# A two-layer decoder trunk on one core: the first stage taken by column quarters with one accumulator each, and residuals of the next projections queued behind the first keys

## The chip, the cores and the metric

The kernel runs on one core of one Trainium2 chip. The metric is the device time of one execution in microseconds (us); before the change it is 693.19 us, the median of 3 runs (692.89 to 694.17).

## The reference, cut to what matters

Two layers over x of shape (1, 256, 1024), all in float32. Each layer is conditioned by `ada = silu(c) @ w_ada + b_ada`, cut into six vectors of 1024 (shift, scale and gate, twice).

```python
def reference(...):
    for l in range(2):
        sh1, sc1, g1, sh2, sc2, g2 = split(silu(c) @ w_ada[l] + b_ada[l], 6)
        h = x * (1.0 + sc1) + sh1
        y = mixer_ab(h, ...) if l == 0 else mixer_cd(h, ...)     # two kinds of attention heads, then @ w_o[l]
        x = layer_norm(ALPHA * x + (1.0 + g1) * y, ln_g[l, 0], ln_b[l, 0])
        h = x * (1.0 + sc2) + sh2
        y = swiglu(h, w_ffn_in[l], w_ffn_out[l])                 # width 2816
        x = layer_norm(ALPHA * x + (1.0 + g2) * y, ln_g[l, 1], ln_b[l, 1])
    return x
```

Layer 0 mixes differential attention (queries q1, keys k1, values v1; a second softmax map is subtracted with a factor lambda made from `diff_lambda`) and dilated window attention (q2, k2, v2). Layer 1 mixes block attention and forgetting attention. All weights, some 160 MB, are read once.

## The kernel before, in words

**Pieces.** Every weight matrix comes in pieces of 128 partitions x 1024 float32 (0.524 MB). The list `stream` holds all of them in the order in which they are to be loaded. `load_ahead` (L76) issues their transfers on SyncE's queue (SP) into a ring of `NR` = 10 raw buffers; `next_piece` (L90) takes the next entry: for a projection weight it makes two tiles by `split` (L72), a rounded copy `hi` (cast on ScalarE, L73) and the residual `lo` (a subtraction on VectorE, L74), and for an `ada` weight it multiplies the piece by a column of silu(c) and adds it to an accumulator on VectorE. Each product of the reference is then three matmuls: hi by hi, lo by hi, hi by lo (`mm3`, L389 to L391, `unit_t_q`, L447 to L449). `piece(name, q)` takes entries until the one asked for is there. After the first stage `room["ring"]` is 7: `pump` takes entries ahead until that many weight pieces are split and not yet used, and `used` pumps again. Those instructions are traced at a lower priority (`high_priority(offset=-LOW)`).

**Order.** Outside of `tc.manual_schedule()` a scheduler orders each engine's instructions by priority and by its own estimate of time; inside, and on SP always, they stay in the order of the program. Engines run their queues in order. Instructions traced later may be put between those of the first stage.

**The first stage** (L607 on) makes h = x(1+sc1)+sh1 and layer 0's v10, q10 and k10 in four quarters q of 256 columns. For a quarter, `first_entries` (L307) streams four pieces of scale and shift weights, each holding two of the eight k of the contraction; VectorE keeps two accumulators, one for even and one for odd k (L317, L319). `first_cols` (L574) sums them over partitions with matmuls against ones (`fin`, L579; two for each of four columns of 128; a float32 matmul shows as two records) and transposes x (`xT`, L585); `first_h` (L589) adds the bias (`column`, L254), forms `hf` on VectorE (L595) and splits it into h. Then come the three projections of that quarter into six PSUM banks, in the order v10, q10 of quarter q, `fin` of q+1, k10 of q, and the splits of v10 of q+1. In `stream` a quarter is four ada pieces, then v10, q10, k10; x and the layer norms' vectors are loaded after the first four pieces, and the small tables, with a bias table, before the last k10. After the fourth quarter `evac_q1` and `evac_k1` copy the queries and keys out of PSUM (the first half of the keys on VectorE, the second on ScalarE, L477), and v1 follows on ScalarE (L636). `bias_vectors` (L557) at the start waits for a table, `kbt`, that ScalarE's queue loads.

**After it**, `attend_diff` (L718) runs layer 0's first attention as 12 steps woven with the projections q20 and k20, two units of six matmuls a step (`weave`). The score banks (0 and 1) are those that held k10. The softmax's exponential is L666 on ScalarE; step s scores map s and makes the softmax of map s-1. `lambdas` (L195) forms lambda before the weave.

**The norm** (`Norm`, L848): `stats` makes the residual sum, its statistics, the reciprocal root on GpSimd (`rsqrt1`, L545) and scales the row's halves, one on ScalarE (L901) and one on VectorE (L902); `turn` transposes, `fill` makes the next h.

Of the kernel before, what the change touches and what calls it, by code (L numbers as in the profile page):

```python
# [2 lines left out]

# [6 lines left out]
F32 = mybir.dt.float32  # L10
# [29 lines left out]
def trunk(ctx, tc, x, c, rel_bias, w_ada, b_ada, ln_g, ln_b, w_in_ab, diff_lambda,  # L40
# [17 lines left out]
    def s4(shape, name, dt=F32):  # L58
# [10 lines left out]
    room = {"ring": 0}  # L69
    at = {"dma": 0, "done": 0, "made": 0, "used": 0}  # L70

    def split(hi, lo, src):  # L72
        A.copy(hi, src)  # L73
        V.tensor_tensor(lo, src, hi.bitcast(F32), OP.subtract)  # L74

    def load_ahead():  # L76
        while at["dma"] < len(stream) and at["dma"] - at["done"] < NR:
# [9 lines left out]
                nc.sync.dma_start(dst, src)  # L87
            at["dma"] += 1

    def next_piece():  # L90

        if at["dma"] == at["done"]:
            load_ahead()
        e = stream[at["done"]]
        if "load" not in e:
            with tc.high_priority(offset=-LOW if room["ring"] else 0):
                if "key" in e:
                    n = "_".join(map(str, e["key"]))
# [6 lines left out]
                    split(hi, lo, e["raw"])  # L105
# [71 lines left out]
    lams = const.tile([128, 2], F32, name="lams")  # L177
    nlam = const.tile([128, 1], F32, name="nlam")

    def load_x():  # L180
        nc.sync.dma_start(rows, b_ada.rearrange("l (i p) -> (l i) p", p=128))
        for t in range(2):
            nc.sync.dma_start(xt[t], x[0, tok(t), :])
        nc.sync.dma_start(lnr[0:32, :], ln_g.rearrange("l i (k p) -> (l i k) p", p=128))
        nc.sync.dma_start(lnr[32:64, :], ln_b.rearrange("l i (k p) -> (l i k) p", p=128))

# [8 lines left out]
    def lambdas():  # L195

        for i in range(2):
            V.scalar_tensor_tensor(lamr[:, 4], lamr[:, 2 * i], 1.0, lamr[:, 2 * i + 1],
                                   OP.mult, OP.mult, accum_out=lams[:, i:i + 1])
# [3 lines left out]
        V.tensor_scalar(subln, subln, 1.0 - LAMBDA_INIT, None, OP.mult)  # L203


    bcol = const.tile([128, 96], F32, name="bcol")
# [100 lines left out]
    def first_entries(q):  # L307
        def work_of(a):
            def go(raw):
                r = raw.rearrange("p (j n) -> p j n", j=2)  # L310
                if a == 0:
                    first[q] = s4([128, 2, 512], f"acc_q{q}")
                for j in range(2):
                    k = 2 * a + j
                    acc = first[q][:, j]
                    if a == 0:
                        V.tensor_scalar(acc, r[:, j], c_sb[:, k:k + 1], None, OP.mult)  # L317
                    else:
# [12 lines left out]
        for a in range(4):  # L331
            stream.append({"work": work_of(a), "dmas": dmas_of(a)})
        for n, c0 in (("v10", 1024), ("q10", 0), ("k10", 512)):
            stream.append(cols_entry(w_in_ab[0], c0, q, n))

    fdw = []

# [33 lines left out]
        stream.extend(rest)  # L371

    for q in range(4):
        first_entries(q)
    stream[4:4] = [{"load": load_x}]
    stream[28:28] = [{"load": load_small}, bias_entry(0)]
    chunk = lambda *ls: [e for l, i in ls for e in ada_entries(l, i)]
    attn0, ffn0 = layer_entries(0)
    attn1, ffn1 = layer_entries(1)
# [20 lines left out]
    def tok(t):  # L400
        return slice(t * 128, t * 128 + 128)
# [63 lines left out]
    def keys(name, E=(A.copy, A.copy)):  # L465

        dst = [s4([128, 4, T], f"{name}{b2}") for b2 in range(2)]
        halves = [d.rearrange("p (b e) t -> p b e t", e=2) for d in dst]
        for d in halves:
            for e in range(2):  # L470
                G.memset(d[64 - e * 64:128 - e * 64, :, e], 0.0)

        def evac(ps, b2):
            p3 = ps.rearrange("p (b t) -> p b t", b=2)
            for e in range(2):
                own = slice(e * 64, e * 64 + 64)
                E[e](halves[b2][own, :, e], p3[own])  # L477

        return dst, evac

# [76 lines left out]
    def bias_vectors():  # L557
        for i in range(2):
# [3 lines left out]
            A.copy(bv, bps[0:8, 0:NV])  # L562
            G.dma_start(vecs[8 * i:8 * i + 8, :], bv)

    h = new_h("00")
    psv = [bank(3, "v10p0"), bank(5, "v10p1")]
    psq = [bank(4, "q10p0"), bank(6, "q10p1")]
    psk = [bank(0, "k10p0"), bank(1, "k10p1")]
# [5 lines left out]
    def first_cols(q):  # L574

        ps = bank(2, f"fin{q}")
        for k in range(4):
            for j in range(2):
                PE.matmul(ps[:, k:k + 1], sums[q][:, j, k * 128:(k + 1) * 128], ones[:, 0:1],  # L579
                          start=j == 0, stop=j == 1)  # L580
        xp = bank(7, f"xT{q}")
        for t in range(2):
            for k in range(2):
                kk = 2 * q + k
                PE.transpose(xp[:, k * 256 + t * 128:k * 256 + t * 128 + 128],  # L585
                             xt[t][:, kk * 128:(kk + 1) * 128], ident)
        return ps, xp

    def first_h(q, ps, xp):  # L589
        column(ps[:, 0:2], 2, 0, 1, 2 * q, f"a{q}")  # L590
        column(ps[:, 2:4], 2, 0, 0, 2 * q, f"b{q}")
        hf = work.tile([128, 2, T], F32, tag="hf", name=f"hf{q}", bufs=2)
        for k in range(2):
            kk = 2 * q + k
            V.tensor_scalar(hf[:, k], xp[:, k * 256:k * 256 + 256], ada[0, 1][:, kk:kk + 1],  # L595
                            ada[0, 0][:, kk:kk + 1], OP.mult, OP.add)
        sl = slice((q % 2) * 2, (q % 2) * 2 + 2)
        split(h[0][q // 2][:, sl], h[1][q // 2][:, sl], hf)

    def qkv(name):  # L600
        return s4([128, 1024], name)
# [3 lines left out]
    k1, evac_k1 = keys("k1", (V.tensor_copy, A.copy))  # L605
    tps = bank(2, "colps")
    with tc.manual_schedule():  # L607
        bias_vectors()
        first_sums(0)
        PE.transpose(tps[:, 0:96], rows, ident[0:96, 0:96])  # L610
        A.copy(bcol, tps[:, 0:96])
        cols = first_cols(0)
        for q in range(4):
            first_h(q, *cols)
            piece("v10", q)
            piece("q10", q)
            for t in range(2):
                run(unit_q(psv[t], "v10", h, t, q, t == 1))
            if q == 3:
# [3 lines left out]
            piece("k10", q)  # L623
            for b2 in range(2):
                run(unit_t_q(psq[b2], "q10", h, b2, q, b2 == 1))
            if q < 3:
                first_sums(q + 1)
                cols = first_cols(q + 1)
                piece("v10", q + 1)
            for b2 in range(2):  # L630
                run(unit_t_q(psk[b2], "k10", h, b2, q, b2 == 1))
        for b2 in range(2):
            evac_q1(psq[b2], b2)
            evac_k1(psk[b2], b2)
        for t in range(2):
            A.copy(v1[:, t], psv[t])  # L636

    room["ring"] = NW // 2
    pump()


    HALF = (slice(0, 128), slice(128, 384))
# [205 lines left out]
    class Norm:  # L848
# [30 lines left out]
        def stats(self, t, ps):  # L879
# [42 lines left out]
        def fill(self, t):  # L922
            for q in range(2):
                hf = work.tile([128, 4, 128], F32, tag="hf", name="hf", bufs=2)
                for k in range(4):
# [121 lines left out]
    for l in range(DEPTH):  # L1047
# [132 lines left out]
```

## Time and profile before

| | |
|---|---|
| runs, median (lowest to highest) | 693.19 us (692.89 to 694.17) |
| the profiled execution, its own time | 693.62 us |
| its span, first to last instruction | 691.6 us |
| TensorE busy | 656.9 us, 95% |
| VectorE busy | 499.8 us, 72% |
| ScalarE busy | 351.3 us, 51% |
| GpSimd busy | 55.2 us, 8% |
| moved by the transfers | 163.21 MB, mean 236 GB/s |

The profile is of one execution. Times are counted from the first instruction of the span. An engine's instructions are named by line, operation and tile; PE is TensorE, DVE VectorE, ACT ScalarE, SP SyncE. The bracket behind an instruction says how long the engine was idle before it and what ended that. A granted clock of 1.00 is 2.4 GHz, 0.50 is 1.2 GHz.

### The profile page before, as it was taken

What the parts mean: (1) busy time and instruction counts of PE and PEld (TensorE: products, weight loads), DVE (VectorE), ACT (ScalarE), POOL (GpSimd) and SP (SyncE); (2) the same over time, 40 slices, a digit from 0 to 9 for tenths busy, and PEclk for the clock granted to TensorE, in tenths of its full rate; (3) what the DMA queues carried; (4) which work ended last, traced back from release to release, by engine and by line L of the source; (5) the groups of instructions that cost most, each with busy time, mean ns of one, the idle gap of its engine ahead of it and who ended that gap; (6) DMA issues with size and microseconds to landing.
All of it is one profiled execution on the core that took longest, in us unless ns stands there. A gap on an engine that the chain in (4) does not pass through costs nothing.

```text
span 691.6 us, 11460 instructions
## 1 busy us (share of the span) xinstructions
PE 656.9 (95%) x4300; PEld 594.4 (86%) x4300; DVE 499.8 (72%) x782; ACT 351.3 (51%) x615; POOL 55.2 (8%) x98
## 2 busy tenths in 40 slices
PE   4899999998999999999999999999799999999994
PEld 2788998877998999999878899978689999999884
DVE  3787999967977787586788868566776558555375
ACT  1426877835544434443557469765564444444330
POOL 4000001011100000000127100100200000000002
PEclk9999999999999999999999999999999999999997
DMA  9999798943899979788846857823466777765101
GB/s 301 360 365 361 250 335 334 343 145 122 305 340 328 321 268 314 225 311 241 271 157 229 297 201 234 280 96 109 140 201 217 225 225 248 238 223 186 32 1 61
DMA packets 96627, 163.21 MB, mean 236 GB/s; under 512 B 8299, under 2 KB 64539, under 8 KB 96572
## 3 DMA queue, kind: packets, MB, share of 16 engines
q1 hardware_dynamic: 95856, 161.82, 70.1%
q8 instruction: 33, 0.54, 0.3%
q10 hardware_dynamic: 524, 0.63, 0.3%
q14 instruction: 22, 0.18, 0.1%
q0 software_dynamic: 192, 0.04, 0.0%
HBM read 161.39 MB, written 1.07 MB: 235 GB/s over the span
## 4 chain that ended last, share of the span: by engine, by line
PE 82%; DVE 7%; DMA 5%; issue 3%; POOL 2%; ACT 1%; DVEq 0%; POOLq 0%; SPq 0%; ACTq 0%
PE gu L432 10%; PE gu L431 10%; PE gu L429 10%; PE f L389 6%; PE f L390 6%; PE f L391 6%; PE gu L389 2%; PE gu L391 2%; PE gu L390 2%; PE y L389 1%; PE y L391 1%; PE y L390 1%; DMA raw<-in_w_ada_dram 1%; PE fin L579 1%; PE adp L279 1%
## 5 line engine op out<-in xcount | busy, mean ns | idle before, releaser
L429 PE MATMUL gu<-h,hifi 128*128 128x256 f32 x576 | 163.0, 283 | 0.0
L431 PE MATMUL gu<-h,hifi 128*128 128x256 f32 x576 | 162.9, 283 | 0.0
L432 PE MATMUL gu<-h,lofi 128*128 128x256 f32 x576 | 162.9, 283 | 0.0
L74 DVE TENSOR_TENSOR lofi<-raw,hifi 128x1024 fp32r<-128x1024 f32 x88 | 105.9, 1220 | 25.8 <-PE gu L431 15.7
L235 DVE SCALAR_TENSOR_TENSOR acc<-raw,c_sb,acc 128x1024 f32<-128x1024 f32 x70 | 89.8, 1285 | 30.0 <-DMA raw<-in_w_ada_dram 29.8
L429 PEld LDWEIGHTS gu<-h,hifi 128*128 128x128 f32 x576 | 110.5, 192 | 0.5
L431 PEld LDWEIGHTS gu<-h,hifi 128*128 128x128 f32 x576 | 110.5, 192 | 0.4
L432 PEld LDWEIGHTS gu<-h,lofi 128*128 128x128 f32 x576 | 110.4, 192 | 0.2
L73 ACT CAST hifi<-raw 128x1024 fp32r<-128x1024 f32 x88 | 91.2, 1048 | 27.5 <-PE y L391 14.0
L389 PE MATMUL f<-hifo,hid 128*128 128x512 f32 (+1 forms) x198 | 74.1, 374 | 0.0
L390 PE MATMUL f<-lofo,hid 128*128 128x512 f32 (+1 forms) x198 | 73.4, 371 | 0.0
L391 PE MATMUL f<-hifo,hid 128*128 128x512 f32 (+1 forms) x198 | 72.9, 368 | 0.0
L73 ACT CAST hifo<-raw 128x1024 fp32r<-128x1024 f32 x44 | 46.2, 1051 | 49.0 <-PE f L391 27.2
L74 DVE TENSOR_TENSOR lofo<-raw,hifo 128x1024 fp32r<-128x1024 f32 x44 | 53.8, 1222 | 5.9 <-PE gu L390 2.4
L978 ACT ACTIVATE sg<-gu 128x256 f32<-128x256 f32 x36 | 13.8, 383 | 79.4 <-PE gu L432 79.4
L548 POOL TENSOR_SCALAR b<-mv 128x1 f32<-128x1 f32 x8 | 6.4, 805 | 466.4 <-DVE mv L894 466.4
L390 PEld LDWEIGHTS f<-lofo,hid 128*128 128x128 f32 x198 | 37.4, 189 | 6.8 <-issue 1.2
L389 PEld LDWEIGHTS f<-hifo,hid 128*128 128x128 f32 x198 | 37.4, 189 | 6.8 <-issue 1.0
L391 PEld LDWEIGHTS f<-hifo,hid 128*128 128x128 f32 x198 | 37.3, 188 | 6.8 <-issue 0.7
L979 DVE TENSOR_TENSOR sg<-gu,sg 128x256 f32<-128x256 f32 x36 | 15.1, 421 | 30.3 <-ACT sg L978 30.3
L389 PE MATMUL gu<-hifi,h 128*128 128x512 f32 x64 | 26.4, 413 | 1.8 <-ACT h L73 1.8
L389 PE MATMUL y<-hiwo,o 128*128 128x512 f32 x64 | 26.5, 416 | 0.0
(352 smaller groups left out, 1438.5 us busy)
## 6 DMA issues: line engine op xcount, KB each, us to landing
raw<-in_w_ffn_in_dram SPq DMA_DIRECT2D x176, 256.0 KB, 4.8
raw<-in_w_ada_dram SPq DMA_DIRECT2D x80, 512.0 KB, 5.2
raw<-in_w_ffn_out_dram SPq DMA_DIRECT2D x44, 512.0 KB, 5.5
raw<-in_w_in_ab_dram SPq DMA_DIRECT2D x24, 512.0 KB, 6.6
raw<-in_w_in_cd_dram SPq DMA_DIRECT2D x24, 512.0 KB, 4.9
raw<-in_w_ada_dram SPq DMA_DIRECT2D x32, 256.0 KB, 6.6
raw<-in_w_o_dram SPq DMA_DIRECT2D x16, 512.0 KB, 5.9
bias<-vecs SPq DMA_DIRECT2D x5, 512.0 KB, 6.7
```

Of the source, the lines that this page charges most:

```text
L73: A.copy(hi, src)
L74: V.tensor_tensor(lo, src, hi.bitcast(F32), OP.subtract)
L235: V.scalar_tensor_tensor(acc, raw, ck, box["z"] if k == 0 else acc, OP.mult, OP.add)
L279: PE.matmul(ps[:, k:k + 1], acc[:, k * 128:(k + 1) * 128], ones[:, 0:1], start=True, stop=True)
L389: PE.matmul(ps, xs[0], ws[0], start=first, stop=False, skip_group_check=True)
L390: PE.matmul(ps, xs[0], ws[1], start=False, stop=False, skip_group_check=True)
L391: PE.matmul(ps, xs[1], ws[0], start=False, stop=last, skip_group_check=True)
L429: PE.matmul(p, wh, hh, start=k == 0 and g == 0, stop=False, skip_group_check=True)
L431: PE.matmul(p, wh, hl, start=False, stop=False, skip_group_check=True)
L432: PE.matmul(p, wl, hh, start=False, stop=k == KT - 1, skip_group_check=True)
L978: A.activation(sg, ps[:, 0:256], AF.Silu)
L979: V.tensor_tensor(sg, ps[:, 256:512], sg, OP.mult)
```

## The change

The diff does the following. (1) A quarter of the first stage keeps one accumulator for all eight k, and from quarter 1 on its first product is a ScalarE activation; `fin` needs four matmuls instead of eight. (2) x is loaded by column quarters, each behind its quarter's ada pieces; k10 of a quarter is streamed a quarter later, and the last k10 comes after the small tables. (3) In a quarter, TensorE now does v10, q10 of q, `fin` of q+1, k10 of q; the transposes stand ahead of `fin`. (4) From quarter 1 on `hf` is made by ScalarE; in quarter 0 h is split by columns of 128 and the v10 residual is queued behind the first of them. The v10 split is taken inside `first_h`. (5) TensorE gets six warming matmuls at the start and two behind the first `fin`. (6) The copies out of PSUM at the end of the stage are put between the last matmuls. (7) After the stage two pieces are pumped freely; the others are traced with `tc.issue_after`, which keeps their VectorE instructions behind the VectorE copy of the second key half. The same is done in layer 1's norms, behind the VectorE scaling of a token half. (8) `lambdas` is called in the second step of the attention.

```diff
+    room = {"ring": 0, "after": None}
+    late = []
-    def split(hi, lo, src):
+    def split(hi, lo, src, now=True):
         A.copy(hi, src)
-        V.tensor_tensor(lo, src, hi.bitcast(F32), OP.subtract)
+        late.append(lambda: V.tensor_tensor(lo, src, hi.bitcast(F32), OP.subtract))
+        if now:
+            late.pop()()
...
-    def next_piece():
+    def next_piece(now=True):
...
-            with tc.high_priority(offset=-LOW if room["ring"] else 0):
+            with tc.high_priority(offset=-LOW if room["ring"] else 0), \
+                    tc.issue_after(room["after"]) if room["after"] else nullcontext():
...
-    def load_x():
+    def load_x(q):
...
+        cs = slice(q * 256, (q + 1) * 256)
         for t in range(2):
-            nc.sync.dma_start(xt[t], x[0, tok(t), :])
+            nc.sync.dma_start(xt[t][:, cs], x[0, tok(t), cs])
+        if q == 2:
+            load_ln()
...
-                    first[q] = s4([128, 2, 512], f"acc_q{q}")
+                    first[q] = s4([128, 512], f"acc_q{q}")
+                acc = first[q]
                 for j in range(2):
                     k = 2 * a + j
-                    acc = first[q][:, j]
-                    if a == 0:
+                    if k == 0 and q:
+                        A.activation(acc, r[:, j], AF.Copy, scale=c_sb[:, k:k + 1])
+                    elif k == 0:
                         V.tensor_scalar(acc, r[:, j], c_sb[:, k:k + 1], None, OP.mult)
...
     for q in range(4):
-        first_entries(q)
-    stream[4:4] = [{"load": load_x}]
-    stream[28:28] = [{"load": load_small}, bias_entry(0)]
+        stream += first_entries(q) + [{"load": lambda q=q: load_x(q)}]
+        for n, c0, k in (("k10", 512, q - 1), ("v10", 1024, q), ("q10", 0, q)):
+            if k >= 0:
+                stream.append(cols_entry(w_in_ab[0], c0, k, n))
+    stream += [{"load": load_small}, bias_entry(0), cols_entry(w_in_ab[0], 512, 3, "k10")]
...
+    def warm(n):
+        for _ in range(n):
+            PE.matmul(wps, ones, ones[:, 0:1].to_broadcast([128, 512]), start=True, stop=True)
...
+        for k in range(4):
+            PE.matmul(ps[:, k:k + 1], sums[q][:, k * 128:(k + 1) * 128], ones[:, 0:1],
+                      start=True, stop=True)
...
         column(ps[:, 2:4], 2, 0, 0, 2 * q, f"b{q}")
+        next_piece(q > 0)
...
+            if q:
+                A.activation(hf[:, k], s, AF.Identity, bias=b, scale=g)
+            else:
+                V.tensor_scalar(hf[:, k], s, g, b, OP.mult, OP.add)
+        for k in range(0, 2, 2 if q else 1):
+            ks = slice(k, 2 if q else k + 1)
+            sl = slice((q % 2) * 2 + ks.start, (q % 2) * 2 + ks.stop)
+            split(h[0][q // 2][:, sl], h[1][q // 2][:, sl], hf[:, ks])
+            while late:
+                late.pop()()
...
+        warm(6)
         bias_vectors()
         first_sums(0)
...
         cols = first_cols(0)
+        warm(2)
+        first_h(0, *cols)
+        piece("q10", 0)
...
         for q in range(4):
...
             for t in range(2):
                 run(unit_q(psv[t], "v10", h, t, q, t == 1))
+            q_units(q)
+            if q < 3:
+                first_sums(q + 1)
+                cols = first_cols(q + 1)
+                piece("k10", q)
+                first_h(q + 1, *cols)
+                piece("q10", q + 1)
+            else:
+                piece("k10", q)
...
+                for b2 in range(2):
+                    evac_q1(psq[b2], b2)
             for b2 in range(2):
                 run(unit_t_q(psk[b2], "k10", h, b2, q, b2 == 1))
+                if q == 3:
+                    keyed = evac_k1(psk[b2], b2)
+                if q == 3 and b2 == 0:
+                    A.copy(v1[:, 0], psv[0])
+        A.copy(v1[:, 1], psv[1])
-    room["ring"] = NW // 2
+    room["ring"] = 2
     pump()
+    room["ring"], room["after"] = NW // 2, keyed.ins
+    pump()
+    room["after"] = None
...
-            V.tensor_scalar(r[:, 0:512], r[:, 0:512], mv[:, 0:1], rstd, OP.subtract, OP.mult)
+            half = V.tensor_scalar(r[:, 0:512], r[:, 0:512], mv[:, 0:1], rstd, OP.subtract,
+                                   OP.mult)
+            if l:
+                room["after"] = half.ins
...
+            if t == 1:
+                room["after"] = None
...
-            lambdas()
+            steps[1] = lambda step=steps[1]: (step(), lambdas())
```

## Rows read from the trace of the kernel before

**Rows 1.** Chain of waits, 0 to 110 us: start, us, what, by count.
```profile
3.74 4.96 DMA kbt<-in_k_bucket_dram
...
23.64 0.43 PE v10p L390
...
28.51 1.68 PE fin L579 x16
...
47.15 0.23 PE v10p L389
...
50.25 0.12 PE q10p L447
...
65.53 0.68 DVE k L477
...
68.70 0.46 PE scA L654 x2
...
100.48 0.86 PE gbp L270 x2
```

**Rows 2.** Stretches: length, busy by engine (instructions), granted clock, DMA share, GB/s.
```profile
0.00:69.00 69.00, 54.70 (x333) 47.61 (x334) 47.50 (x78) 24.98 (x34) 10.35 (x25) 0.98 1.02 347
...
25.20:35.30 10.10, 10.10 (x79) 9.72 (x78) 7.49 (x12) 3.59 (x5) 1.04 (x2) 1.00 1.08 362
...
42.60:45.80 3.20, 3.20 (x17) 3.20 (x16) 1.83 (x4) 1.74 (x3) 0.77 (x2) 0.50 1.06 371
...
69.00:80.00 11.00, 11.00 (x88) 10.69 (x86) 9.87 (x34) 10.27 (x29) 0.00 (x0) 1.00 0.70 222
80.00:100.00 20.00, 20.00 (x169) 19.85 (x168) 19.93 (x42) 14.13 (x40) 0.00 (x0) 1.00 0.90 306
100.00:120.00 20.00, 20.00 (x101) 16.13 (x100) 19.48 (x51) 15.34 (x37) 2.35 (x3) 1.00 0.92 348
120.00:140.00 20.00, 20.00 (x107) 16.73 (x107) 18.16 (x31) 15.38 (x40) 0.00 (x0) 1.00 1.03 351
140.00:150.00 10.00, 10.00 (x61) 8.85 (x61) 5.56 (x12) 1.04 (x1) 1.88 (x3) 1.00 0.23 78
```

**Rows 3.** VectorE in order of time, first stage: start, us, line, out<-in.
```profile
10.74 1.42 DVE L319 SCALAR_TENSOR_TENSOR acc_q<-raw,c_sb,acc_q 128x512 f32<-128x512 f32 x2 [0.30 <-DMA raw<-in_w_ada_dram]
...
23.64 4.07 DVE L319 SCALAR_TENSOR_TENSOR acc_q<-raw,c_sb,acc_q 128x512 f32<-128x512 f32 x6
...
30.73 0.99 DVE L595 TENSOR_SCALAR hf<-xT,col,col 128x256 f32<-128x256 f32 x2 [0.27 <-PE xT L585]
32.41 0.69 DVE L74 TENSOR_TENSOR h<-hf,h 128x512 fp32r<-128x512 f32 x1 [0.69 <-ACT h L73]
33.36 1.23 DVE L74 TENSOR_TENSOR loq<-raw,hiq 128x1024 fp32r<-128x1024 f32 x1 [0.26 <-ACT hiq L73]
...
43.03 1.00 DVE L595 TENSOR_SCALAR hf<-xT,col,col 128x256 f32<-128x256 f32 x2 [0.49 <-PE xT L585]
```

**Rows 4.** ScalarE in order of time, first stage.
```profile
25.20 1.05 ACT L73 CAST hiv<-raw 128x1024 fp32r<-128x1024 f32 x1 [3.91 <-DMA raw<-in_w_in_ab_dram]
...
35.28 1.05 ACT L73 CAST hiv<-raw 128x1024 fp32r<-128x1024 f32 x1 [1.00 <-DMA raw<-in_w_in_ab_dram]
...
57.72 1.28 ACT L200 ACT_TABLE_LOAD   x1
...
67.97 0.58 ACT L477 COPY k<-k10p 64x512 f32<-64x512 f32 x1 [0.39 <-DVE k L477]
```

**Rows 5.** VectorE in order of time, layer 1's first norm.
```profile
480.52 1.22 DVE L74 TENSOR_TENSOR lofi<-raw,hifi 128x1024 fp32r<-128x1024 f32 x1
...
482.97 1.18 DVE L74 TENSOR_TENSOR lofi<-raw,hifi 128x1024 fp32r<-128x1024 f32 x1
```

**Rows 6.** TensorE in order of time, around 40 and 487 us.
```profile
39.98 0.35 PE L579 MATMUL fin<-ones,acc_q 128*128 128x1 f32 x2 [0.80 <-DVE acc_q L319]
...
486.71 0.44 PE L920 MATMUL xnT100v<-ident,x 128*128 128x128 f32 x2 [1.88 <-DVE x L902]
```

More of the change, by code (lines that the diff above doesn't have):

```diff
@@ L1 @@
 import math
-from contextlib import ExitStack
+from contextlib import ExitStack, nullcontext
 import concourse.bass as bass
@@ L68, in trunk @@
              ("fo1", 2 * NU - 1)}
-    room = {"ring": 0}
+    room = {"ring": 0, "after": None}
     at = {"dma": 0, "done": 0, "made": 0, "used": 0}
-    def split(hi, lo, src):
+    late = []
+    def split(hi, lo, src, now=True):
         A.copy(hi, src)
-        V.tensor_tensor(lo, src, hi.bitcast(F32), OP.subtract)
+        late.append(lambda: V.tensor_tensor(lo, src, hi.bitcast(F32), OP.subtract))
+        if now:
+            late.pop()()
     def load_ahead():
@@ L104, in next_piece @@
                         at["made"] += 1
-                    split(hi, lo, e["raw"])
+                    split(hi, lo, e["raw"], now)
                     pieces[e["key"]] = (hi, lo)
@@ L178, in trunk, with load_ln @@
     nlam = const.tile([128, 1], F32, name="nlam")
-    def load_x():
-        nc.sync.dma_start(rows, b_ada.rearrange("l (i p) -> (l i) p", p=128))
+    def load_x(q):
+        if q == 0:
+            nc.sync.dma_start(rows, b_ada.rearrange("l (i p) -> (l i) p", p=128))
+        cs = slice(q * 256, (q + 1) * 256)
         for t in range(2):
-            nc.sync.dma_start(xt[t], x[0, tok(t), :])
+            nc.sync.dma_start(xt[t][:, cs], x[0, tok(t), cs])
+        if q == 2:
+            load_ln()
+    def load_ln():
         nc.sync.dma_start(lnr[0:32, :], ln_g.rearrange("l i (k p) -> (l i k) p", p=128))
@@ L197, in lambdas @@
         for i in range(2):
-            V.scalar_tensor_tensor(lamr[:, 4], lamr[:, 2 * i], 1.0, lamr[:, 2 * i + 1],
-                                   OP.mult, OP.mult, accum_out=lams[:, i:i + 1])
+            tc.keep_in_program_order(
+                V.scalar_tensor_tensor(lamr[:, 4], lamr[:, 2 * i], 1.0, lamr[:, 2 * i + 1],
+                                       OP.mult, OP.mult, accum_out=lams[:, i:i + 1]))
         A.activation(lams, lams, AF.Exp)
@@ L202, in lambdas @@
                                OP.subtract)
-        V.tensor_scalar(subln, subln, 1.0 - LAMBDA_INIT, None, OP.mult)
+        tc.keep_in_program_order(V.tensor_scalar(subln, subln, 1.0 - LAMBDA_INIT, None, OP.mult))
     bcol = const.tile([128, 96], F32, name="bcol")
@@ L329, in dmas_of @@
                 for g, i in enumerate((1, 0))]
[L331 to L334, printed above, removed]
+        return [{"work": work_of(a), "dmas": dmas_of(a)} for a in range(4)]
     fdw = []
@@ L476, in evac @@
                 own = slice(e * 64, e * 64 + 64)
-                E[e](halves[b2][own, :, e], p3[own])
+                done = E[e](halves[b2][own, :, e], p3[own])
+                if e == 0:
+                    first = done
+            return first
         return dst, evac
@@ L563, in bias_vectors @@
             G.dma_start(vecs[8 * i:8 * i + 8, :], bv)
+    def warm(n):
+        for _ in range(n):
+            PE.matmul(wps, ones, ones[:, 0:1].to_broadcast([128, 512]), start=True, stop=True)
     h = new_h("00")
+    wps = bank(3, "warm")
     psv = [bank(3, "v10p0"), bank(5, "v10p1")]
@@ L576, in first_cols @@
         ps = bank(2, f"fin{q}")
[L577 to L580, printed above, removed]
         xp = bank(7, f"xT{q}")
@@ L594, in first_h @@
             kk = 2 * q + k
[L595 to L598, printed above, removed]
+            s, g, b = xp[:, k * 256:k * 256 + 256], ada[0, 1][:, kk:kk + 1], ada[0, 0][:, kk:kk + 1]
+            if q:
[8 more added lines that the diff above has]
+                late.pop()()
     def qkv(name):
@@ L612, in trunk, with q_units @@
         cols = first_cols(0)
+        warm(2)
+        first_h(0, *cols)
+        piece("q10", 0)
+        def q_units(q):
+            for b2 in range(2):
+                run(unit_t_q(psq[b2], "q10", h, b2, q, b2 == 1))
         for q in range(4):
-            first_h(q, *cols)
-            piece("v10", q)
-            piece("q10", q)
             for t in range(2):
                 run(unit_q(psv[t], "v10", h, t, q, t == 1))
-            if q == 3:
+            q_units(q)
[7 more added lines that the diff above has]
+                piece("k10", q)
                 tps = bank(7, "lnps")
@@ L622, in trunk @@
                 A.copy(lncol, tps[:, 0:64])
[L623 to L629, printed above, removed]
+                for b2 in range(2):
+                    evac_q1(psq[b2], b2)
             for b2 in range(2):
                 run(unit_t_q(psk[b2], "k10", h, b2, q, b2 == 1))
[L632 to L636, printed above, removed]
-    room["ring"] = NW // 2
+                if q == 3:
[4 more added lines that the diff above has]
+    room["ring"] = 2
     pump()
+    room["ring"], room["after"] = NW // 2, keyed.ins
+    pump()
+    room["after"] = None
     HALF = (slice(0, 128), slice(128, 384))
```

## The prediction

> **What bounds the kernel now.** I read the page's slices first, then busy time by stretch, then the chain of waits, then the queues of VectorE, ScalarE and TensorE in order of time. TensorE is busy 95% of the span, and its idle time lies at the front: 54.70 us busy in the first 69, then 71 of 71 up to 140 [rows 2]. So what is worth asking is when layer 0's attention starts. Its first score pair needs a PSUM bank that still holds the last key sums; the chain shows the second pair starting at 68.70 [rows 1]. From there TensorE is the bound, and a start earlier by d us ends the run d earlier, if VectorE and the transfers keep up.
>
> Up to there, two things run side by side. The transfers are saturated: 347 GB/s over the first 69 us, 362 GB/s at a DMA share above 1 in 25.2 to 35.3 [rows 2]. ScalarE waits for data only at two value pieces, at 25.20 and 35.28 [rows 4]. Between those two arrivals lie seven pieces of 128x1024 f32 (0.524 MB): 3.67 MB in 10.08 us, 0.364 MB/us, 1.44 us a piece. At that pace the first stage's data would be in by 50 us, 19 before it ends. The rest is the order of work: per quarter VectorE does two first products, six accumulations (4.07), three residuals (1.22 each, 1.14 apart), `hf` (0.99) and its residual (0.69) [rows 3], about 10.3 us with the columns, and its waits for ScalarE and TensorE make it 12.3 (`hf` at 30.73, the next at 43.03). TensorE also has 16 one-column records for `fin` (1.68 in quarter 1 [rows 1]).
>
> **First stage, the data.** I count the new order in pieces of 1.44 us, taking x's quarter as half a piece and anchoring on the old order, in which v10 of quarter 1 is the 14th piece and there at 25.1. Then in the new order: weights of ada quarter 1 complete at 20.1, k10 of quarter 0 at 22.2, ada quarter 2 at 30.9, k10 of 1 at 33.0, ada quarter 3 at 41.7, k10 of 2 at 43.8, v10 of 3 at 45.3, q10 of 3 at 46.7. The small loads and a bias table follow (1.35 pieces), so the last, k10 of 3, lands at 50.1, and the four q20 pieces at 51.5 to 55.9. Cutting x into eight transfers adds six issues of about 0.4 us on SP, which is issuing seven or more pieces ahead by then: nothing.
>
> **First stage, the engines.** A quarter is 7.5 pieces, 10.8 us of transfer. TensorE's share of it: 24 matmuls for k and 24 for q at 0.12 (2.88 each), 12 for v at 0.23 (2.76) [rows 1], `fin` now 8 records instead of 16 (1.68/2, so 0.84), transposes 0.5 (from that `fin`'s end at 30.19 to `hf` at 30.73 [rows 3]): 9.9. VectorE, from a key piece's landing: cast 1.04 [rows 4], residual 1.22, columns 0.25 (an estimate: within that same gap), v residual 1.14, a wait of about 0.15 for `hf` and its cast on ScalarE (two 256-column activations, each at most the 0.58 of a 512-column copy [rows 4], beside the v residual), 0.69, q residual 1.14, seven accumulations of 0.68 (4.75): 10.4, so the sums stand 0.4 before the next key piece. The single accumulator makes each step wait for the one before; bounds: nothing, or 0.1 a step, 0.7 a quarter; I take nothing, as the instructions already follow each other closely [rows 3]. All three fit below 10.8, so the transfers are the bound, by 0.4 us.
>
> The end then: k10 of 2 lands 43.8, cast 44.85, residual 46.1; k on TensorE to 49.0 (the last `h` is there at 48.6, only 0.4 early), v to 51.75, q to 54.6, the norm vectors' transpose 0.3 (an estimate: half of x's), k of 3 (landed and split by 52.4) to 57.8; key copies on VectorE 0.68 [rows 1] and behind it on ScalarE 0.58 [rows 4]; second score pair at 59.3. Against 68.70: **9.4 us earlier**. Quarter 0 is hidden under this: its accumulation ends at 12.16 as before [rows 3], and its matmuls by 22, where the sums of quarter 1 are due. The six warming matmuls cost 0.86 each at 2.4 GHz (as `gbp` [rows 1]), so 1.72 at 1.2; all six slow would hold the bias vectors 2.6 us beyond their table's landing at 8.70 [rows 1]. TensorE would then be up to 3 late into quarter 1 and win back 0.9 in each later one: 0 to 1.1, I take 0.
>
> **Clock.** In 42.6 to 45.8 the granted clock is 0.50, 1.2 GHz [rows 2], after TensorE had waited 0.80 for the sums and gone through `fin` [rows 6]. That drop cost half of 3.2, 1.6 us. Quarter 0 also runs v at 0.43 a matmul (1.2 GHz) [rows 1]. The change leaves a wait of about 1.2 us per quarter between `fin` and k. A drop in quarters 1 and 2 is mostly absorbed by the 0.9 of slack; one in quarter 3 is paid in full, 1.6. I take half of that: **+0.8**, ends 0 and 3.0 (three drops of 1.6, less twice 0.9).
>
> **Hand-over.** The exponential's table load (1.28 at 57.72 [rows 4]) moves from inside the stage to the first softmax. TensorE has projection units until the third step; 0 to 1.28, I take 0.3. Behind the keys' VectorE copy now queue all residuals but two: q20's third and fourth (1.22 each) would be done by 62.5 with the first softmaxes between them, and TensorE wants the third about 62.9 (score pair, then two pieces of 1.44): hidden, 0 to 2.4 if not. Behind those wait `k20`'s residuals, due 9 us later.
>
> **Layer 0's attention, 69 to 140 before.** VectorE is busy 9.87+19.93+19.48+18.16 = 67.4 of 71 [rows 2]. It now gets two q20 residuals that lay before (2.3) and the lambda (0.7): 70.4 in 71. What can slip: in 140 to 150 it is busy only 5.56 and the transfers fall to 78 GB/s [rows 2], so work and data run ahead of need by then. On bytes: the rates times their stretches give 46.5 MB by 140 [rows 2]; the new kernel has some 20.6 of them at 59.3 and would need 25.9 more in 71 us, 74 at the 350 GB/s of the last rows. Give-back 0 to 3; I take **+0.7**, near the lower end because TensorE shows no idle there.
>
> **Layer 1's norm.** `room["after"]` is set at the first token half's scaling and holds later residuals behind it. Before, one at 480.52 takes 1.14 inside the statistics and one at 482.97 lies in the wait for the reciprocal root; TensorE waits 1.88 for the scaled rows [rows 5, 6]. The first goes: -1.1. Both then fall into the busier stretch behind the scaling: 0 to +2.3. I take **-0.9**, ends -1.9 and +1.2.
>
> **Sum**, on the profiled execution (693.62, span 691.6): -9.4+0.8+0.3+0.7-0.9 = -8.5, 685.1. The runs' median, 693.19, is 0.43 below the profiled execution: 684.7, forecast **684.8 us**.
>
> **Rivals.**
> *The clock falls in every quarter*, because TensorE now waits on transfers. For: the drop at 42.6. Against: two other quarters have as much `fin` and no drop. 3.0 in place of 0.8: 687.0.
> The Trainium skill, "TensorE: Matmul & The Clock Gate", section "HAM oscillation", says that waits for transfers between bursts of matmuls bring the low clock back each time; it speaks against this order. The trace bears it out once in the four quarters [rows 2].
> *Part of it is given back in layer 0's attention*: q20 late (2.4) and transfers (3) instead of 0.7, less what overlaps, about +4: 688.8. For: VectorE at 95% there. Against: no TensorE wait there now.
> *Slower*: VectorE's fixed order in that stretch meets data that come later relative to its users, and stalls in order. 70.4 us of work must then take more than 80, a busy share under 88%; now it is 95%, in the first stage it is 47.50 of 69, 69% [rows 2]. At 84% the stretch takes 83.8, 12.5 longer: 696.6.
> *It doesn't do what it says*: the scheduler still puts casts of q20 and k20 ahead of ScalarE's key copies, where they wait for data until about 60, and VectorE keeps its 12.3 us a quarter: about 692.5. Against: the stage's order is written out by hand.
>
> **Numbers.** Forecast 0.52 (682.5 to 686.5 by itself), better than that 0.07 (no drop, the norm's full gain), clock 0.17, give-back 0.13, no effect 0.05, slower 0.06. Runs here can tell 0.2% (1.4 us) from no change. Faster 0.88, same 0.06, slower 0.06. Range 681.0 to 689.5: it leaves out the slower cases, part of the give-back and a little below.
>
> **What would show it.** Second score pair near 59 to 61; k10 of 2 cast near 44; `fin` 8 records, a quarter every 10.8 us, ScalarE waiting for data at the key pieces; no key copy held by a cast; TensorE without idle from 60 to 131. Wrong if the quarters stay at 12 us, if TensorE waits in `q20p`, or if the norm of layer 1 shows a longer wait.

## The result, and the profile after

The changed kernel takes **684.74 us** (median of 4 runs, 683.03 to 686.21), the kernel before, beside it, 693.68 (692.89 to 694.21): ratio 0.9866, 95% interval 0.9844 to 0.9888, 8.9 us faster. The forecast was 684.8. A second measurement gave 683.56 against 694.35, 10.8 us faster (below), so the gain is known to some 2 us. The profiled execution of the changed kernel is its fastest, 683.03, so the trace shows a little more gain (10.6 against 693.62) than the medians.

The page of the changed kernel, head and busy times:

```profile
span 681.3 us, 11437 instructions
...
PE 656.1 (96%) x4284; PEld 588.8 (86%) x4284; DVE 499.6 (73%) x774; ACT 356.6 (52%) x625; POOL 55.5 (8%) x98
```

ScalarE in order of time: the casts of the key pieces. They answer to [rows 4]; the wait for data now stands at the keys.

```profile
22.42 1.05 ACT L76 CAST hik<-raw 128x1024 fp32r<-128x1024 f32 x1 [3.77 <-DMA raw<-in_w_in_ab_dram]
...
34.48 1.05 ACT L76 CAST hik<-raw 128x1024 fp32r<-128x1024 f32 x1 [4.91 <-DMA raw<-in_w_in_ab_dram]
...
45.31 1.04 ACT L76 CAST hik<-raw 128x1024 fp32r<-128x1024 f32 x1 [4.95 <-DMA raw<-in_w_in_ab_dram]
```

VectorE over one whole quarter, from key residual to key residual, then the first key copy; they answer to [rows 3] and to the copy in [rows 1]:

```profile
35.56 1.23 DVE L77 TENSOR_TENSOR lok<-raw,hik 128x1024 fp32r<-128x1024 f32 x1
36.80 0.23 DVE L267 SCALAR_TENSOR_TENSOR col<-fin,bcol 128x2 f32<-128x2 f32 x2
36.94 1.22 DVE L77 TENSOR_TENSOR lov<-raw,hiv 128x1024 fp32r<-128x1024 f32 x1
38.83 0.69 DVE L77 TENSOR_TENSOR h<-hf,h 128x512 fp32r<-128x512 f32 x1 [0.67 <-ACT h L76]
39.78 1.23 DVE L77 TENSOR_TENSOR loq<-raw,hiq 128x1024 fp32r<-128x1024 f32 x1 [0.25 <-ACT hiq L76]
40.92 5.47 DVE L334 SCALAR_TENSOR_TENSOR acc_q<-raw,c_sb,acc_q 128x512 f32<-128x512 f32 x7
46.39 1.23 DVE L77 TENSOR_TENSOR lok<-raw,hik 128x1024 fp32r<-128x1024 f32 x1
...
58.06 0.68 DVE L491 COPY k<-k10p 64x512 f32<-64x512 f32 x1 [1.42 <-PE k10p L463]
```

A quarter is 10.83 us where it was 12.3 (from `hf` to `hf`). Two things are to be seen. The seven accumulations take 5.47, 0.78 each: every one reads what the one before wrote; in [rows 3], with two accumulators in turn, six took 4.07, 0.68 each. And the residual of h waits 0.67 for ScalarE. At 46.39 VectorE goes from its last accumulation to the key residual with no wait at all, although that key's cast began only at 45.31, when its data came: engine and transfer arrive together.

TensorE: `fin` of quarters 0 and 2, the warming matmuls between, and the scaled rows of layer 1's first norm (they answer to [rows 1, 6]):

```profile
12.48 1.83 PE L607 MATMUL fin<-ones,acc_q 128*128 128x1 f32 x8 [0.40 <-DVE acc_q L334]
14.18 3.76 PE L585 MATMUL warm<-ones 128*128 128x512 f32 x4
...
35.73 1.02 PE L607 MATMUL fin<-ones,acc_q 128*128 128x1 f32 x8 [0.74 <-DVE acc_q L334]
...
474.49 0.44 PE L966 MATMUL xnT100v<-ident,x 128*128 128x128 f32 x2 [0.79 <-DVE x L945]
```

Stretches (length, busy by engine in the order PE, PEld, DVE, ACT, POOL, granted clock, DMA share, GB/s), to set against [rows 2]:

```profile
8.00:20.00 12.00, 10.22 (x30) 5.37 (x30) 8.41 (x14) 4.50 (x8) 4.66 (x7) 0.72 1.07 343
...
40.00:50.00 10.00, 9.26 (x68) 8.61 (x68) 9.13 (x13) 4.51 (x7) 0.00 (x0) 1.00 1.07 365
...
70.00:80.00 10.00, 10.00 (x83) 9.80 (x82) 10.00 (x29) 8.00 (x24) 0.00 (x0) 1.00 0.96 353
80.00:100.00 20.00, 19.88 (x132) 17.29 (x131) 19.57 (x33) 14.99 (x36) 2.35 (x3) 1.00 0.98 357
100.00:120.00 20.00, 20.00 (x112) 17.43 (x111) 19.46 (x52) 17.32 (x49) 0.00 (x0) 1.00 0.84 304
120.00:140.00 20.00, 20.00 (x114) 16.86 (x114) 16.09 (x25) 8.58 (x17) 0.00 (x0) 1.00 0.89 299
```

The attention is as dense as before. Where the gain stands along the run, in starts of TensorE's instructions (us, from the tile views; "no key rule" and the last column are experiments told below):

| station | before | after | no key rule | half ada, two accumulators, addition |
|---|---|---|---|---|
| first score pair | 67.1 | 59.5 | 63.7 | 57.3 |
| last q20 matmul | 86.7 | 78.2 | 83.9 | 76.0 |
| layer 0, norm 1, first half turned | 151.4 | 144.0 | 149.7 | 141.8 |
| the same, second half | 165.9 | 157.6 | 162.1 | 155.4 |
| forget gate of layer 1 (`lfT`) | 393.3 | 385.1 | 391.3 | 383.2 |
| layer 1, norm 1, first half turned | 486.7 | 474.5 | 481.9 | 474.3 |
| span | 691.6 | 681.3 | 688.9 | 680.6 |

8.5 us are won by the end of q20, and 8.2 are still there at 385. A second profile of the kernel before had its `lfT` at 395.4 instead of 393.3, having run at 0.91 in 160 to 180 us where the first one had 1.00, so differences behind the first layer are good to some 2 us.

### The profile page after: what moved, and what is told of

It is laid out like the page before. It is cut to its first block, busy times and chain, and to the rows that moved or that the text cites. A ratio compares the mean times of both kernels' runs of the same rounds, so it can differ in the third digit from the quotient of the medians.

```text
span 681.3 us, 11437 instructions
## 1 busy us (share of the span) xinstructions
PE 656.1 (96%) x4284; PEld 588.8 (86%) x4284; DVE 499.6 (73%) x774; ACT 356.6 (52%) x625; POOL 55.5 (8%) x98
## 4 chain that ended last, share of the span: by engine, by line
PE 77%; DVE 9%; DMA 6%; issue 3%; POOL 2%; ACT 2%; SPq 0%; DVEq 0%; POOLq 0%; ACTq 0%
PE gu L446 10%; PE gu L445 10%; PE gu L443 10%; PE f L403 6%; PE f L404 6%; PE f L405 6%; DMA raw<-in_w_ada_dram 3%; PE gu L405 1%; PE gu L404 1%; PE gu L403 1%; DVE acc_q L334 1%; PE y L404 1%; PE y L403 1%; PE adp L292 1%; PE y L405 1%
## 5 line engine op out<-in xcount | busy, mean ns | idle before, releaser
L76 ACT CAST hifi<-raw 128x1024 fp32r<-128x1024 f32 x88 | 91.3, 1048 | 20.8 <-PE gu L446 10.3
```

## The experiments

Theory A, that of the prediction: the transfers set the quarter, VectorE's chain would need 10.4. Theory B: VectorE's chain sets it. "The front" is the work up to the first scores. The runs were taken on three chips, on which the kernel before took 694.35 us (up to the norm rule), 694.09 (from the key rule on) and 695.81 (the last three experiments). The changed kernel itself was measured again on the first of them only, so the others are compared by their ratio to the kernel before.

**The changed kernel a second time.** No edit.

> The changed kernel once more, on the chip of the next three. Its runs so far lie between 683.0 and 686.2: expect a median of 684 to 685.5, and a profile in which the stage's stations (fourth quarter's key cast, first and second score pair) lie within 0.3 us of the first profile, while stations behind 390 us may differ by the 1.6 us of a clock drop that is there in one execution and not in another.

683.56 us, ratio 0.9845 [0.9831, 0.986], somewhat under what was expected, with the same stations within 0.3 us up to 385.

**Two accumulators again**, with both first products of quarters 1 to 3 on ScalarE and 16 records of `fin`.

```diff
-first[q] = s4([128, 512], f"acc_q{q}")
+first[q] = s4([128, 2, 512], f"acc_q{q}")
...
-    PE.matmul(ps[:, k:k + 1], sums[q][:, k * 128:(k + 1) * 128], ..., start=True, stop=True)
+    for j in range(2):
+        PE.matmul(ps[:, k:k + 1], sums[q][:, j, k * 128:(k + 1) * 128], ..., start=j == 0, stop=j == 1)
```

> The changed kernel with two accumulators a quarter again, for even and odd k (both first products on ScalarE from quarter 1 on, six accumulations on VectorE, 16 records of fin). Everything else as changed. Theory A, the transfers set the quarter (as predicted): VectorE's shorter chain only waits longer for the key piece; score pairs at the same place or up to 0.8 later for the longer fin, 684.7 to 685.5. Theory B, VectorE's chain sets it: seven chained accumulations take 5.47 in the changed kernel, six in turns took 4.07 before, so each of three quarters gets 1.4 shorter, less 0.84 of fin where that is not hidden: score pairs 1.5 to 3.5 earlier, 681.5 to 683.5.

683.36 us, 0.9846 [0.9828, 0.9864]: no difference in time, though the first score pair comes 1.3 later (60.8). VectorE in order of time, then TensorE:

```profile
31.60 4.06 DVE L334 SCALAR_TENSOR_TENSOR acc_q<-raw,c_sb,acc_q 128x512 f32<-128x512 f32 x6
...
38.20 0.23 DVE L267 SCALAR_TENSOR_TENSOR col<-fin,bcol 128x2 f32<-128x2 f32 x2 [1.41 <-PE fin L608]
...
46.30 1.23 DVE L77 TENSOR_TENSOR lok<-raw,hik 128x1024 fp32r<-128x1024 f32 x1
```

```profile
36.32 1.84 PE L608 MATMUL fin<-ones,acc_q 128*128 128x1 f32 x16
```

VectorE saves 1.4 on the accumulations and pays it back waiting for `fin`, which takes 1.84 on TensorE; the quarter stays at 10.7. What the single accumulator costs VectorE it saves on TensorE, which is now busy without a gap (10.00 of 10 us in 40 to 50). The 1.3 lost at the front are won back later: the first half of layer 1's norm is turned at 474.4, in the changed kernel at 474.5. So the single accumulator by itself brings no time that can be measured.

**Half of the ada data**: two pieces in place of four in quarters 1 to 3.

```diff
+if q:
+    def both(a):
+        g0, g1 = work_of(a), work_of(a + 2)
+        return lambda raw: (g0(raw), g1(raw))
+    return [{"work": both(a), "dmas": dmas_of(a)} for a in range(2)]
```

> The changed kernel, but in quarters 1 to 3 only the first two of the four ada pieces are loaded and each is multiplied twice, so that 1.05 MB (two pieces, 2.9 us of transfer) a quarter are not moved; every instruction of VectorE, ScalarE and TensorE stays (the scale and shift of these quarters are made from other numbers). Theory A, the transfers set the quarter: the stage's end moves forward until the next bound, VectorE's chain without its waits, 10.2 a quarter or less: 1.5 to 3 us in all, 682 to 683.5. Theory B, VectorE's chain sets it: at most the first wait of quarter 1 goes, 0 to 0.5, 684 to 685.

683.69 us, 0.9846 [0.9831, 0.9861]. ScalarE, then VectorE:

```profile
29.81 1.04 ACT L76 CAST hik<-raw 128x1024 fp32r<-128x1024 f32 x1
...
40.61 1.04 ACT L76 CAST hik<-raw 128x1024 fp32r<-128x1024 f32 x1
```

```profile
35.84 1.22 DVE L77 TENSOR_TENSOR lok<-raw,hik 128x1024 fp32r<-128x1024 f32 x1
...
46.64 1.22 DVE L77 TENSOR_TENSOR lok<-raw,hik 128x1024 fp32r<-128x1024 f32 x1
```

The key's cast is done 5 us ahead of its residual, and the residuals are still 10.80 apart. So VectorE's chain by itself needs 10.8: theory A, that only the transfers do, falls.

**Without the rule at layer 1's norm.**

```diff
-if l:
-    room["after"] = half.ins
```

> The changed kernel without the rule in layer 1's norms (the later residuals are again free to lie inside the norm's VectorE work). The prediction's term is 0.9: expect the wait for the scaled rows back at 1.9 instead of 0.8, and 685.5 to 686.5. If the gain at this place in the profile (2 us and no clock drop behind it) is the rule's, 686.5 to 688. If it is chance of the order, no difference from the changed kernel.

685.18 us, 0.9875 [0.9854, 0.9896], 1.6 above the second run of the changed kernel on the same chip, with intervals that just overlap. VectorE, TensorE, then a stretch of it and the same one of the changed kernel:

```profile
471.02 1.22 DVE L77 TENSOR_TENSOR lofi<-raw,hifi 128x1024 fp32r<-128x1024 f32 x1
...
473.47 1.17 DVE L77 TENSOR_TENSOR lofi<-raw,hifi 128x1024 fp32r<-128x1024 f32 x1
```

```profile
477.22 0.44 PE L964 MATMUL xnT100v<-ident,x 128*128 128x128 f32 x2 [1.88 <-DVE x L945]
```

```profile
480.00:485.00 5.00, 4.93 (x15) 3.98 (x16) 4.95 (x7) 4.95 (x7) 0.00 (x0) 0.66 0.08 15
```

```profile
480.00:485.00 5.00, 5.00 (x24) 4.14 (x23) 4.51 (x6) 2.71 (x4) 1.41 (x2) 1.00 0.38 113
```

Both residuals are back where [rows 5] had them, TensorE's wait is 1.88 again, as in [rows 6], and behind it the clock falls to 0.66; with the rule it is 1.00 in the same stretch. This is no chance of one execution: in all ten profiles with the rule the wait is 0.8 and the clock 1.00 in the 8 us from 1 us behind the turning, in all three without it (this one and the two of the kernel before) the wait is 1.9 and the clock 0.62 to 0.79. The rows are turned (transposed) 2.7 later, of which 0.6 was there at the scores of layer 1 already, and the span is 1.3 longer: with the rule TensorE waits 1.63 for the second half of the rows, without it it does not.

**Without the key rule**: all residuals may stand ahead of the key copies.

```diff
-room["ring"] = 2
-pump()
-room["ring"], room["after"] = NW // 2, keyed.ins
+room["ring"] = NW // 2
 pump()
-room["after"] = None
```

> The changed kernel without the two-step pump: all seven pieces may be split at once after the first stage, their VectorE residuals free to lie ahead of the key copies. If the rule is what brings the scores forward: key copies wait on VectorE for up to two more residuals (1.2 each), second score pair 1 to 2.4 later, 685 to 686.5. If the data set it (q20's third piece is only cast near 55.7, its fourth near 59.9): the residuals find VectorE free or come too late, no difference, 683.3 to 685.

689.42 us, 0.993 [0.9903, 0.9956]: about half of the gain is gone, outside both expectations. TensorE's waits from 20 to 140 us, then ScalarE and VectorE around the key copies:

```profile
PE scA L694 <- ACT k L491: 3.8, 1, 3.8
```

```profile
59.89 1.04 ACT L76 CAST hik<-raw 128x1024 fp32r<-128x1024 f32 x1 [0.36 <-PE k10p L463]
...
61.91 1.05 ACT L76 CAST hik<-raw 128x1024 fp32r<-128x1024 f32 x1
62.98 0.58 ACT L491 COPY k<-k10p 64x512 f32<-64x512 f32 x1
```

```profile
55.50 5.29 DVE L77 TENSOR_TENSOR loq<-raw,hiq 128x1024 fp32r<-128x1024 f32 x4
60.96 1.22 DVE L77 TENSOR_TENSOR lok<-raw,hik 128x1024 fp32r<-128x1024 f32 x1 [0.18 <-ACT hik L76]
62.11 0.67 DVE L491 COPY k<-k10p 64x512 f32<-64x512 f32 x1
```

All four residuals of q20 and one of k20 go ahead of VectorE's first key copy, two casts of k20 ahead of ScalarE's; the first copy comes at 62.11 instead of 58.06, and TensorE stands still for 3.8. By the table, the first score pair is 3.4 earlier than before without the rule and 7.6 with it: in this kernel the rule brings 4.2 of it (the wait, and keys that are done 0.4 earlier), and 5.7 of the 8.5 at the end of q20: behind the wait the clock is 0.57 in 64 to 68 us. The other 3.4 belong to the rest of the change. Of that, the single accumulator and the warming were taken out by themselves (1.3 above, 0.9 below); the order of the loads, ScalarE's share and the place of the copies were not.

**Without the warming matmuls.**

```diff
-warm(6)
...
-warm(2)
```

> The changed kernel without any of the eight warming matmuls. Prediction: quarter 0 is covered, 0 to 1.1 us; the v10 and q10 matmuls of quarter 0 run at 1.2 GHz. Since VectorE's chain, and no longer the transfers, is what half the ada pieces less showed to set the quarters, a delay of fin in quarters 0 or 1 is not won back: then 0.5 to 2.5 later, 684.3 to 686.5.

686.49 us, 0.9892 [0.9863, 0.992]. The key residual of quarter 1 comes at 36.48 against 35.56, because the columns ahead of it wait 0.64 for a TensorE that is late from quarter 0; the first key copy is 0.94 later. `fin` of quarter 0 takes 1.84, as with the warming, so what the warming brings is faster matmuls behind it. The rest of what its profile shows (the slowest of the six executions, span 686.5) lies far behind, in the wait for the forget gate, 3.0 instead of 1.7, and a stretch after it:

```profile
387.50:393.50 6.00, 6.00 (x27) 5.02 (x28) 4.13 (x6) 1.53 (x2) 3.27 (x4) 0.50 0.91 320
```

6 us at half clock cost 3 by estimate. This stretch is slow in some executions of one kernel and not in others: the two profiles of the kernel before differ in it too (below). So it is not put down to the edit, and beyond the 0.94 no cost of leaving the warming out is shown.

**Lambda formed early.**

```diff
-steps[1] = lambda step=steps[1]: (step(), lambdas())
+lambdas()
```

> The changed kernel with lambda formed where it was before, ahead of the weave. Prediction's term: 0.3, from the table load of 1.28 that now stands before the first softmax. If the scheduler puts it back into the stage: VectorE's chain there gets 0.8 longer at the most, the softmax starts 1.3 earlier. Expect no difference that can be measured, 683 to 685.

685.16 us, 0.9885 [0.9855, 0.9914], which cannot be told from the change. Written earlier, lambda was scheduled later: its last product runs at 75.7 instead of 64.9. What lambda costs ahead of the scores stays untested.

**The kernel before a second time.** No edit, one execution.

> The kernel before, a second profile, to see whether the half clock in layer 1's keys (the stretch of 393 to 400 us of its first profile) and in the first gate matmuls behind layer 1's norm (489.5 to 493.5) comes each time. Theory: both come from what TensorE does just before, so they come again, and their absence in the changed kernel's profiles is an effect of the moved work. Rival: chance of one execution; then one of them is missing here.

694.11 us. A stretch behind the forget gate, in the first profile and in this one:

```profile
396.00:400.00 4.00, 4.00 (x29) 3.43 (x28) 2.88 (x6) 0.00 (x0) 0.66 (x2) 0.83 0.92 307
```

```profile
396.00:400.00 4.00, 4.00 (x34) 3.57 (x33) 3.80 (x6) 1.53 (x2) 3.73 (x4) 1.00 0.94 341
```

And one of this profile behind layer 1's norm:

```profile
490.00:495.00 5.00, 4.79 (x14) 3.85 (x15) 4.81 (x7) 4.95 (x7) 0.00 (x0) 0.63 0.08 8
```

Behind the forget gate the low clock of the first profile (0.75 in 392 to 396, 0.83 in 396 to 400) is missing here, so it is chance of one execution. Behind layer 1's norm it came again (0.70 in the same stretch of the first profile): there its absence in the changed kernel is an effect of the change, and the run without the norm's rule shows that it is the rule's.

**Two accumulators, brought together by one addition**, so that VectorE's chain gets shorter and `fin` keeps 8 records.

```diff
+if q:
+    V.tensor_tensor(first[q][:, 0], first[q][:, 0], first[q][:, 1], OP.add)
+sums[q] = first[q][:, 0]
```

> In quarters 1 to 3 two accumulators alternate again, with both first products on ScalarE, and one VectorE addition (128x512) brings them together, so fin keeps its 8 records. VectorE's chain of a quarter loses 5.47 and gets six steps of 0.68 (4.06) and an addition of about 0.69: 10.8 becomes 10.1, and TensorE, which idled 0.74 a quarter behind fin, needs about 10.06 as well. If VectorE's chain alone sets the quarter, the key residuals come every 10.1 us, the key copies 0.7 times 3, so some 2 us, earlier than 58.06, and the time falls by up to 2 us, to about 681.5. If the transfers set it just as much (they ran at a DMA share above 1 all the while, and the third key piece landed at 45.2 with VectorE free for it at the same moment), the key pieces land at 34.4 and 45.2 as before, the residuals stay 10.8 apart, ScalarE and VectorE wait longer for the keys, and the time stays within 0.5 us of 683.4.

685.72 us, 0.986 [0.9835, 0.9884]: by the ratio no gain (the 683.4 of the expectation is from another chip). ScalarE, then VectorE:

```profile
34.28 1.04 ACT L76 CAST hik<-raw 128x1024 fp32r<-128x1024 f32 x1 [4.87 <-DMA raw<-in_w_in_ab_dram]
...
45.09 1.05 ACT L76 CAST hik<-raw 128x1024 fp32r<-128x1024 f32 x1 [4.42 <-DMA raw<-in_w_in_ab_dram]
```

```profile
33.62 0.69 DVE L338 TENSOR_TENSOR acc_q<-acc_q 128x512 f32<-128x512 f32 x1
35.36 1.23 DVE L77 TENSOR_TENSOR lok<-raw,hik 128x1024 fp32r<-128x1024 f32 x1 [1.05 <-ACT hik L76]
...
46.17 1.23 DVE L77 TENSOR_TENSOR lok<-raw,hik 128x1024 fp32r<-128x1024 f32 x1 [0.77 <-ACT hik L76]
```

VectorE is done early and waits 1.05 and 0.77 for the key, whose data land where they did, at 365 GB/s and a DMA share of 1.08 in 40 to 50 us. So the transfers need 10.8 too: theory B, that only VectorE does, falls as well.

**The same with half of the ada data**, both edits together.

> The same two accumulators and addition, and the data taken away: in quarters 1 to 3 only two of the four ada pieces are loaded and each is multiplied twice, so scale and shift are made from other numbers. Without the addition this lack of data left the quarter at 10.8 us. If VectorE's chain and the transfers both stand at 10.8, only here, where both are shortened, do the key residuals come every 10.1 us, with the first key copy near 56 and the time 1.5 to 2 us under that of the kernel with the addition alone. If VectorE's chain alone counts, this kernel and the one with the addition alone agree within 0.5 us. If something else holds the quarter (ScalarE, or TensorE at 10.8), both stay at 10.8.

680.74 us, 0.9781 [0.9752, 0.9809]. VectorE, then a stretch of all engines:

```profile
24.00 1.22 DVE L77 TENSOR_TENSOR lok<-raw,hik 128x1024 fp32r<-128x1024 f32 x1
...
34.06 1.22 DVE L77 TENSOR_TENSOR lok<-raw,hik 128x1024 fp32r<-128x1024 f32 x1
...
44.17 1.22 DVE L77 TENSOR_TENSOR lok<-raw,hik 128x1024 fp32r<-128x1024 f32 x1
...
55.89 0.68 DVE L498 COPY k<-k10p 64x512 f32<-64x512 f32 x1 [2.83 <-PE k10p L470]
```

```profile
40.00:50.00 10.00, 9.95 (x73) 9.29 (x72) 8.97 (x14) 5.61 (x8) 0.00 (x0) 1.00 1.05 384
```

Only with both shortened do the residuals come every 10.1 us, and the front is 2.2 earlier. TensorE is then busy 9.95 of 10 us, so it would be the next bound. The medians differ by 5.0, more than expected; the profiled execution, the slowest of its four at 682.49, shows the 2.2 at 157 us and nearly none of it at 474. Behind the forget gate its clock is 0.79 in 380 to 388 us, where the changed kernel has 1.00, which by estimate is 1.7 of 8 us. Where the other executions win more than 2.2 is not shown.

**Three more warming matmuls between the bias vectors and the first `fin`.**

```diff
+warm(2)
 PE.transpose(tps[:, 0:96], rows, ident[0:96, 0:96])
+warm(1)
```

> Three more warming matmuls are put between the bias vectors and the first fin (two ahead of the transpose of the bias rows, one behind it), into the 0.70 and 0.40 us in which TensorE waited there and in which the clock fell. If the clock then stays up, fin of quarter 0 takes about 0.85 instead of 1.83, the first columns come 0.9 earlier, at about 13.6, and VectorE starts quarter 1 that much earlier. If VectorE's chain alone sets the quarters, all later stations move 0.9 earlier: about 682.6. If the transfers set them too, the key pieces land as before and the time stays within 0.3 us of 683.4. If three matmuls at the low clock hold up fin instead, it is 0.5 to 1 us slower.

685.96 us, 0.987 [0.9847, 0.9892]: nothing gained. TensorE:

```profile
12.13 1.05 PE L585 MATMUL warm<-ones 128*128 128x512 f32 x2
13.46 0.95 PE L607 MATMUL fin<-ones,acc_q 128*128 128x1 f32 x8
```

`fin` takes 0.95 instead of 1.83, so the clock is up; but it begins 0.98 later, behind three matmuls that take 3.04 together, more than the waits they were to fill: the last of the outcomes named. The `fin` of quarter 1 comes at 25.99 instead of 24.91.

Of the versions that leave nothing out, none is measurably faster than the changed kernel.

## Why the prediction was right

**First stage, the engines: the step that failed.** "All three fit below 10.8, so the transfers are the bound, by 0.4 us." The 10.4 held the key's cast, 1.04, which lies beside the last accumulations on ScalarE; VectorE's own part was 9.3, and it is 10.8. The accumulations cost 5.47, not 4.75: the upper bound named for the chained accumulator, 0.7 a quarter, is what it costs, and nothing was taken. The wait for h is 0.67, not 0.15, and the 0.25 for q's cast was left out: 1.5 in all. The forecast did not suffer, because the transfers really need 10.8 as well, and the larger of two equal bounds is the same number. That was luck: nothing in the prediction held VectorE to 10.8. Only the kernel with both shortened shows that there are two bounds. TensorE has 0.74 to spare a quarter ahead of `fin` (not behind it, as an expectation above has it), so its 10.06 agrees with the 9.9.

**First stage, the data.** Key pieces were to land at 22.2, 33.0 and 43.8 and were waited for until 22.42, 34.48 and 45.31: right at first and for the last interval, 1.3 too long in between. What lengthens that one was not isolated. The sum -9.4+0.8+0.3 stands at -8.3 for front, clock and hand-over; -8.5 is measured at the end of q20. The last keys on TensorE are done at 59.5 instead of 57.8. So 0.9 of the 9.4 is missing, for which the late data are the only cause seen, and the 1.1 added for clock and hand-over were not paid: two errors that cancel.

**Clock.** In quarters 1 to 3 the granted clock is 1.00 although TensorE waits in each; the 0.8 was not paid. It fell where none was counted, to 0.72 in 8 to 20 us, and `fin` of quarter 0 took 1.83. That cost at most 0.2: with VectorE early, the key residual still came at 35.36 instead of 35.56, held by its data. The Trainium skill, "TensorE: Matmul & The Clock Gate", section "HAM oscillation", tells of a kernel whose waits for transfers between bursts bring the low clock back each time. Those waits are several times as long as the ones here, so the section did not speak against this order, as the prediction has it. By the row of 40 to 50 us the clock stays at 1.00 behind waits of 0.74.

**Hand-over.** q20's fourth cast does stand ahead of ScalarE's second key copy (60.94), and the second score pair starts at 62.07, not 59 to 61; but TensorE does q20 in between and has no idle time: 0 where 0.3 was taken. The rival "it doesn't do what it says" named the mechanism that matters most, casts (and, as the run without the key rule shows, residuals) ahead of key copies. It was priced as part of a failure, not as a term; its removal is worth 4.2 at the first score pair.

**Layer 0's attention.** Give-back 0.7: the gain is 8.5 at the end of q20, 7.4 when the first half is turned, 8.3 at the second. About 1 was given back and returned, so 0.2 stands where 0.7 was taken.

**Layer 1's norm.** -0.9 was taken; 1.3 (spans) to 1.6 (medians) is what taking the rule away costs. The sum left out two things: behind the longer wait the clock falls, 0.66 in the stretch without the rule, and with the rule TensorE waits 1.63 for the second half of the rows.

**Where the trace shows more than was predicted**, from 8.2 at 385 to 9.7 at the scores of layer 1 (445.7 to 436.0), the kernel before ran a stretch at 0.75 there that its other profile did not have. Against that other profile the gain is 10.3 at both places. This is not the change's doing.

**The sum.** As measured, the terms are -8.5 for the front, 0.2 given back and -1.3 to -1.6 for the norm, together some -9.7 where -8.5 was forecast. The medians give -8.9 in one measurement and -10.8 in the other. So the forecast gain was a little small, and that 684.8 stands so close to 684.74 is luck: the same kernel's other median is 683.56. The premise that a start earlier by d ends the run d earlier holds to some 2 us only: in the profiles, the 1.3 that two accumulators lose at the front and the 2.2 that the shortest quarters win there are both nearly gone at layer 1's norm.

The slower case did not occur: VectorE did the 60 us from 80 to 140 with 55.12 busy, without holding up TensorE by more than 0.12.

## What to carry to other kernels

When one stage is cut, work out every engine's chain and the transfers for the new order and say by how much the largest leads; if two come out within half a microsecond, only shortening both will show which bound is left. An accumulation that reads its own last result on VectorE is to be priced at its chained pace. And a rule that keeps prepared work behind the first instruction that somebody waits for can be worth as much as the reordering it goes with (4.2 of 7.6 us here at the first scores): ask what stands in each queue ahead of that instruction.

## What was not expected of the hardware

VectorE's multiply-add of 128x512 f32 follows itself every 0.78 us when it reads the sum just written and every 0.68 when two sums alternate (5.47 for seven, 4.06 for six). TensorE's half clock behind the forget gate's wait comes in some executions of a kernel and not in others, and not by the length of the wait: in the two profiles of the kernel before, 0.75 was granted after a wait of 1.5 us and 1.00 after one of 1.8. And at the start of an execution the granted clock does not show the level: without the warming matmuls it reads 1.00 in 8 to 20 us, while v10 takes 0.43 a matmul there and 0.23 later.
